# The second group of hidden column tiles in program order, its pairs' work in four steps, and two norm row operations placed later

## The chip, the core and the metric

The kernel runs on one core of a Trainium2 chip. The metric is the device time of one execution in microseconds (us). Four engines work here: TensorE (PE in the profile; its weight loads are PEld), VectorE (DVE), ScalarE (ACT) and GpSimd (POOL, almost idle). SyncE (SP) issues the loads. Each engine runs its own instructions in their order and waits on semaphores for the others.

## The reference

One encoder layer on 256 tokens of width 2048 in float32: attention, cross-attention to 256 memory tokens, and an MLP, each followed by a layer norm. The change lies in the MLP and at its entrance:

```python
x = layer_norm(ALPHA * x + xa, ln2_g[l], ln2_b[l])
ff = squared_relu_mlp(x, w_mlp_in[l], w_mlp_out[l])   # square(relu(h @ w_in)) @ w_out
x = layer_norm(ALPHA * x + ff, ln3_g[l], ln3_b[l])
```

The MLP's hidden width is 8192, that is 64 column tiles of 128.

## The kernel before, in words

**Splits.** Every float32 operand is split into a high and a low half: ScalarE copies the source to `hi` (in the reduced format that TensorE multiplies), VectorE subtracts to get `lo` (lines 87 and 88; in the stage studied, `queued_split` at lines 947 to 949). A product takes three matmuls, hi·hi, hi·lo and lo·hi (`mm3`, lines 164 to 166). Weights arrive in 1 MB loads (`raw`), and each load becomes two halves of 128x1024, each with its own pair of splits. `w_hi` has four buffers and `lo` four fixed ones, so a split also waits until TensorE has used the buffer four halves back.

**The groups.** The first eight column tiles of the hidden layer are computed ahead, in two groups of four (`hidden_group`, line 970). A group goes over the 16 row tiles k of the width; `cols_wide` (line 208) issues, for each k, four matmuls of 128x512 with `hi` (line 213) and four of 128x256 with `lo` (line 218). One half of a load covers two values of k. Group 1 writes the four `acc` tiles, group 2 the four `att` tiles. After a group its tiles are emptied (`evacuate`, lines 870 and 871), and two tiles make a **pair** p. `finish` applies relu (879) and the square (880) to a pair and splits it into `ht` (874, 875); `pair_sums` makes three sums of its quarters on VectorE (891, 894, 895) and splits those into `aux` (874, 875).

**The passes.** After that the kernel runs passes over (chunk c, half q). A pass alternates a **g** item (`hidden_tile`, lines 1004 and 1012: one more column tile of the hidden layer, 16 wide and 16 narrow matmuls) with a **u** item (a pair multiplied into the output, seven products by a Strassen scheme, 21 matmuls at lines 164 to 166, on four splits: two from `raw`, two from the sums `s_t` that line 941 makes). In the first pass the order is g8, g9, u0, g10, u1, g11, u2, g12, and so on; u0 and u1 use the pairs of group 1, u2 and u3 those of group 2.

**What sets the order.** `queue` (line 100) ties an instruction behind the last one queued on its engine. Splits of the groups and passes are queued on ScalarE and VectorE, and the g and u matmuls on TensorE. Before the change the matmuls of group 2 are in free order: a scheduler places them. Work beside the splits stands in the list `side`; `pump` (line 110) takes entries from it, two after each half in group 2, and in the passes one after each split that has no sum of `s_t` to make. The entries of group 1 are: four empty ones, two evacuations, then `finish` and `pair_sums` of each pair as whole entries, then four row operations `norm_ops(0)` (line 1174: the layer norm's gain, then its bias, on the residual, 128x1024 each, for two row blocks). Those of group 2 are two evacuations, `finish`, `pair_sums`, `finish`, `pair_sums`, taken up in g8 and u0. `norm_rows` (1168) loads the gain and bias rows into `row_b`, again with the other half of the columns once the first four row operations are done.

```python
    side.extend([lambda i=i, h=h: empty(i, h) for i, h in pairs])
    for i, h in pairs:
        side.append(lambda i=i, h=h: finish(h, c, j0 // 2 + i, queue))
        side.append(lambda i=i, h=h: pair_sums(h, c, j0 // 2 + i, queue))
```

Of the kernel before, what the change touches and what calls it, by code (L numbers as in the profile page):

```python
# [14 lines left out]
AF = mybir.ActivationFunctionType  # L15
# [3 lines left out]
P = 128  # L19
S = 256  # L20
D = 2048
KT = D // P
# [11 lines left out]
CH = 16  # L34
# [4 lines left out]
def encoder_kernel(ctx: ExitStack, tc: tile.TileContext, t, out):  # L39
    nc = tc.nc  # L40
# [29 lines left out]
    def tmp_tile():  # L70
        return rings["tmp"].tile([P, 512], F32, tag="tmp", name="tmp")
# [10 lines left out]
    def pin(ins, pinned):  # L82
        return tc.keep_in_program_order(ins) if pinned else ins
# [18 lines left out]
    side, banks, fixed_lo = deque(), deque(), deque()  # L102
# [105 lines left out]
    def cols_wide(outs, hi, lo, xt, k, nk, pinned=False):  # L208


        def his():
            for i, ps in enumerate(outs):
                pin(nc.tensor.matmul(ps, hi[:, i * P:(i + 1) * P], xt[:, k, :],  # L213
                                     start=k == 0, stop=k == nk - 1), pinned)

        def los():
            for i, ps in enumerate(outs):
                pin(nc.tensor.matmul(ps[:, 0:S], lo[:, i * P:(i + 1) * P], xt[:, k, 0:S],
                                     start=False, stop=False), pinned)

        for part in ((los, his) if k == nk - 1 else (his, los)):
            part()
# [99 lines left out]
    class Heads:  # L322
# [11 lines left out]
        def finish(self):  # L334
            while self.live:
                self.step()
# [515 lines left out]
    def take(what, c, p):  # L852
        place[what, c, p] = free[what].pop(0)
# [19 lines left out]
    def ordered_split(hi, lo, src, to):  # L873
        to(nc.scalar.activation(hi, src, AF.Copy))
        to(nc.vector.tensor_tensor(out=lo, in0=src, in1=f(hi), op=ALU.subtract))

    def finish(h, c, p, to=free_order):

        to(nc.scalar.activation(h, h, AF.Relu))
        to(nc.scalar.activation(h, h, AF.Square))  # L880
        take("h", c, p)
        x = hid(c, p)
        ordered_split(x[:, :, 0:S], x[:, :, S:2 * S], h.rearrange("p (i c) -> p i c", c=S), to)

    def pair_sums(h, c, p, to=free_order):

        if p in SEVEN:
            a11, a21, a12, a22 = [h[:, o:o + P] for o in range(0, 4 * P, P)]
            s = tmp_tile()
            s3, s1, s2, s4 = [s[:, o:o + P] for o in range(0, 4 * P, P)]  # L890
            to(nc.vector.tensor_tensor(out=s[:, 0:2 * P].rearrange("p (i c) -> p i c", c=P),
                                       in0=a21[:, None, :].broadcast_to([P, 2, P]),
                                       in1=h.rearrange("p (i c) -> p i c", c=P)[:, 0:4:3, :], op=ALU.subtract))
            to(nc.vector.tensor_tensor(out=s2, in0=s1, in1=a11, op=ALU.subtract))
            to(nc.vector.tensor_tensor(out=s4, in0=a12, in1=s2, op=ALU.add))
            take("s", c, p)
            y = sums_of(c, p)
            ordered_split(y[:, 0, :], y[:, 1, :], s, to)

    raws, raw_of, fetched, sums = [raw_x], {}, [0], deque()  # L900
    items = []
# [68 lines left out]
    def hidden_group(nexts, tiles, c, j0, beside=None):  # L970

        outs = [tiles() for _ in range(G)]
        for k in range(0, KT, 2):
            hi, lo = nexts(k)
            for i in range(2):
                cols_wide(outs, hi[:, i * G * P:(i + 1) * G * P], lo[:, i * G * P:(i + 1) * G * P],
                          x2t, k + i, KT, beside is not None)
            if beside is not None:
                beside(k // 2)
        if j0 + G == LEAD:  # L980
            for _ in range(3):
                fetch()
        pairs = [(i // 2, tmp_tile()) for i in range(0, G, 2)]

        def empty(i, h):
            for j in range(2):
                evacuate(outs[2 * i + j], h, j, queue)

        side.extend([lambda i=i, h=h: empty(i, h) for i, h in pairs])
        for i, h in pairs:  # L990
            side.append(lambda i=i, h=h: finish(h, c, j0 // 2 + i, queue))
            side.append(lambda i=i, h=h: pair_sums(h, c, j0 // 2 + i, queue))

    now, late_finish = [], []

    def hidden_tile(it, ps):

        _, c, j = it
        for h_ in range(2):
            hi, lo = part(raw_of[it][:, h_ * 1024:(h_ + 1) * 1024])  # L1000
            k0 = 8 * h_

            def w_hi(k):
                queue(nc.tensor.matmul(ps, hi[:, k * P:(k + 1) * P], x2t[:, k0 + k, :],  # L1004
                                       start=k0 + k == 0, stop=k0 + k == KT - 1))
# [12 lines left out]
        evacuate(ps, now[0], j % 2)  # L1018
        if j % 2:
            def rest(h=now[0]):  # L1020
                last = j == CH - 1
                finish(h, c, j // 2, queue if last else free_order)
                pair_sums(h, c, j // 2)
            late_finish.append(rest)

    bank = []
# [139 lines left out]
    def norm_rows(q):  # L1166
        for i, w in enumerate("gb"):
            nc.sync.dma_start(row_b[:, i * 1024:(i + 1) * 1024],
                              t[f"ln2_{w}"][q * 1024:(q + 1) * 1024].partition_broadcast(P))

    def norm_ops(q):
        o = q * 1024
        return [lambda i=i, b=b, op=op: queue(
            nc.vector.tensor_tensor(out=res[b][:, o:o + 1024], in0=res[b][:, o:o + 1024],
                                    in1=row_b[:, i * 1024:(i + 1) * 1024], op=op))
            for i, op in enumerate((ALU.mult, ALU.add)) for b in range(NB)]

    for g in range(LEAD // G):
        hidden_group((lambda k: w_mi0[k // 2]) if g == 0 else (lambda k: s_in.next()),
                     att_tile if g % 2 else acc_tile, 0, g * G, first_pair if g == 0 else None)  # L1180
        if g == 0:
# [150 lines left out]
```

## Time and profile before

| | |
|---|---|
| median of 3 runs | 1109.28 us (1107.59 to 1109.54) |
| the profiled execution's own time | 1109.07 us |
| its span | 1107.3 us |
| TensorE busy | 98% of the span |
| VectorE busy | 85% |
| ScalarE busy | 58% |
| group 2, g8, g9, u0, g10, u1 | 423.28 to 487.87 us |

The times of the trace count from the start of the span. A timeline row gives the start, the duration from the first to the last end of what it merges, the engine, the line, the operation, output and inputs, a count, and in brackets the idle time of the engine just before and what ended it. Durations of neighbours overlap, because the engines are pipelined: what an instruction costs its engine is the distance from its start to the next start. A windows row gives for one stretch the busy time of each engine, the granted TensorE clock (1.00 is full), the share of the DMA engines and GB/s.

### The profile page before, as it was taken

What the parts mean: (1) busy time and instruction counts of PE and PEld (TensorE: products, weight loads), DVE (VectorE), ACT (ScalarE), POOL (GpSimd) and SP (SyncE); (2) the same over time, 40 slices, a digit from 0 to 9 for tenths busy, and PEclk for the clock granted to TensorE, in tenths of its full rate; (3) what the DMA queues carried; (4) which work ended last, traced back from release to release, by engine and by line L of the source; (5) the groups of instructions that cost most, each with busy time, mean ns of one, the idle gap of its engine ahead of it and who ended that gap; (6) DMA issues with size and microseconds to landing.
All of it is one profiled execution on the core that took longest, in us unless ns stands there. A gap on an engine that the chain in (4) does not pass through costs nothing.

```text
span 1107.3 us, 15277 instructions
## 1 busy us (share of the span) xinstructions
PE 1082.2 (98%) x5864; PEld 932.2 (84%) x5864; DVE 936.7 (85%) x1299; ACT 638.5 (58%) x925; POOL 38.2 (3%) x45
## 2 busy tenths in 40 slices
PE   9999999999999999889999999999999999999996
PEld 6988899988999877768888888888888888888885
DVE  6878677687889676899999999899999899999876
ACT  6555566545576425566566566566666566666540
POOL 1402000000100000000000000000000000000000
PEclk9999999999999999999999999999999999999998
DMA  9664453466567334645566556556655555645742
GB/s 332 235 228 143 156 194 124 178 218 244 184 200 277 140 113 152 228 152 198 193 217 228 195 186 226 192 190 209 210 190 195 211 192 197 226 167 196 256 147 77
DMA packets 37369, 215.87 MB, mean 195 GB/s; under 512 B 4272, under 2 KB 5168, under 8 KB 13616
## 3 DMA queue, kind: packets, MB, share of 16 engines
q1 hardware_dynamic: 37296, 214.89, 54.7%
q8 instruction: 46, 0.75, 0.3%
q14 instruction: 27, 0.22, 0.1%
HBM read 212.78 MB, written 2.10 MB: 194 GB/s over the span
## 4 chain that ended last, share of the span: by engine, by line
PE 89%; DVE 6%; ACT 2%; DMA 2%; issue 1%; SPq 0%; POOL 0%; DVEq 0%; ACTq 0%
PE acc L164 12%; PE acc L165 12%; PE acc L166 12%; PE acc L1004 11%; PE acc L1012 6%; PE att L1004 6%; PE att L165 4%; PE att L166 4%; PE att L164 4%; PE att L1012 3%; PE acc L206 2%; PE acc L205 2%; PE acc L204 2%; DVE lo L949 2%; PE acc L213 1%; PE att L213 1%
## 5 line engine op out<-in xcount | busy, mean ns | idle before, releaser
L87 ACT ACTIVATE w_hi<-raw 128x1024 fp32r<-128x1024 f32 (+2 forms) x134 | 131.6, 989 | 114.1 <-PE acc L166 73.3
L88 DVE TENSOR_TENSOR w_lo<-raw,w_hi 128x1024 fp32r<-128x1024 f32 (+2 forms) x130 | 146.0, 1132 | 59.5 <-ACT w_hi L87 58.5
L949 DVE TENSOR_TENSOR lo<-raw,w_hi 128x1024 fp32r<-128x1024 f32 (+1 forms) x154 | 171.2, 1128 | 6.2 <-ACT w_hi L948 5.9
L948 ACT ACTIVATE w_hi<-raw 128x1024 fp32r<-128x1024 f32 (+1 forms) x154 | 147.5, 982 | 29.4 <-PE acc L166 27.0
L1004 PE MATMUL acc<-x2t,w_hi 128*128 128x512 f32 x592 | 153.6, 391 | 1.5 <-ACT w_hi L948 1.4
L1004 PEld LDWEIGHTS acc<-x2t,w_hi 128*128 128x128 f32 x592 | 108.8, 189 | 21.7 <-ACT w_hi L948 2.1
L949 DVE TENSOR_TENSOR lo<-s_t,w_hi 128x1024 fp32r<-128x1024 f32 x84 | 102.5, 1220 | 12.0 <-ACT w_hi L948 12.0
L948 ACT ACTIVATE w_hi<-s_t 128x1024 fp32r<-128x1024 f32 x84 | 88.8, 1057 | 35.2 <-PE acc L1004 11.8
L1012 PEld LDWEIGHTS acc<-x2t,lo 128*128 128x128 f32 x592 | 80.7, 190 | 5.8
L165 PE MATMUL acc<-lo,ht 128*128 128x512 f32 x213 | 82.9, 389 | 0.0
L1012 PE MATMUL acc<-x2t,lo 128*128 128x256 f32 x592 | 82.5, 282 | 0.0
L164 PE MATMUL acc<-w_hi,ht 128*128 128x512 f32 x210 | 82.0, 391 | 0.2 <-DVE res L1075 0.2
L166 PE MATMUL acc<-w_hi,ht 128*128 128x512 f32 x210 | 81.8, 389 | 0.0
L1004 PE MATMUL att<-x2t,w_hi 128*128 128x512 f32 x304 | 78.4, 391 | 0.0
L870 ACT ACTIVATE tmp<-acc 128x256 f32<-128x256 f32 x41 | 15.6, 388 | 102.1 <-PE acc L1004 95.2
L165 PE MATMUL acc<-w_lo,xt 128*128 128x512 f32 (+2 forms) x192 | 69.4, 363 | 0.6 <-DVE w_lo L88 0.6
L166 PE MATMUL acc<-w_hi,xt 128*128 128x512 f32 (+2 forms) x192 | 69.1, 361 | 0.0
L164 PE MATMUL acc<-w_hi,xt 128*128 128x512 f32 (+2 forms) x192 | 65.7, 362 | 0.7 <-ACT w_hi L87 0.7
L1004 PEld LDWEIGHTS att<-x2t,w_hi 128*128 128x128 f32 x304 | 55.8, 189 | 10.0
L949 DVE TENSOR_TENSOR lo<-raw_x,w_hi 128x1024 fp32r<-128x1024 f32 (+1 forms) x50 | 55.2, 1122 | 2.4 <-ACT w_hi L948 2.4
L164 PE MATMUL att<-w_hi,aux 128*128 128x512 f32 x131 | 51.3, 392 | 2.5 <-ACT w_hi L948 2.3
L165 PE MATMUL att<-lo,aux 128*128 128x512 f32 x131 | 51.3, 392 | 2.1 <-DVE lo L949 2.1
(293 smaller groups left out, 2505.7 us busy)
## 6 DMA issues: line engine op xcount, KB each, us to landing
raw<-in_w_mo SPq DMA_DIRECT2D x41, 1024.0 KB, 4.9
raw<-in_w_mc SPq DMA_DIRECT2D x34, 1024.0 KB, 4.9
raw<-in_w_out SPq DMA_DIRECT2D x16, 1024.0 KB, 4.8
raw_x<-in_w_mc SPq DMA_DIRECT2D x13, 1024.0 KB, 4.8
raw_x<-in_w_mo SPq DMA_DIRECT2D x13, 1024.0 KB, 4.9
row_b<-in_w_mo SPq DMA_DIRECT2D x10, 1024.0 KB, 4.8
row_b<-in_w_mc SPq DMA_DIRECT2D x9, 1024.0 KB, 4.9
raw<-in_w_mi SPq DMA_DIRECT2D x8, 1024.0 KB, 5.0
```

The source lines that it names most:

```text
L87: pin(nc.scalar.activation(hi, src, AF.Copy), pinned)
L88: return pin(nc.vector.tensor_tensor(out=lo, in0=src, in1=f(hi), op=ALU.subtract), pinned)
L164: keep(nc.tensor.matmul(ps, ah, bh, start=start, stop=False))
L165: keep(nc.tensor.matmul(ps, ah, bl, start=False, stop=False))
L166: keep(nc.tensor.matmul(ps, al, bh, start=False, stop=stop))
L204: nc.tensor.matmul(ps, hi, xt[:, k, 0:S], start=k == 0, stop=False)
L205: nc.tensor.matmul(ps, hi, xt[:, k, S:2 * S], start=False, stop=False)
L206: nc.tensor.matmul(ps, lo, xt[:, k, 0:S], start=False, stop=k == nk - 1)
L948: queue(nc.scalar.activation(hi, src, AF.Copy))
L949: queue(nc.vector.tensor_tensor(out=lo, in0=src, in1=f(hi), op=ALU.subtract))
L1004: queue(nc.tensor.matmul(ps, hi[:, k * P:(k + 1) * P], x2t[:, k0 + k, :], start=k0 + k == 0, stop=k0 + k == KT - 1))
L1012: queue(nc.tensor.matmul(ps[:, 0:S], lo[:, k * P:(k + 1) * P], x2t[:, k0 + k, 0:S], start=False, stop=False))
```

## The change

1. The matmuls of group 2 are queued from its third row tile on (k > 1), and the last row tile of group 1, which was only kept in program order, is queued as well. TensorE therefore runs the rest of group 1 before the rest of group 2, and the whole of group 2 before g8.
2. `finish` and `pair_sums` become four steps, `square`, `halve`, `add` and `halve_sums`, and these are listed by hand: in group 1 one entry after another with the two gain row operations among the last; in group 2 a list whose entries hold up to two steps.
3. The two bias row operations move from group 2 behind group 2's own pairs, which puts them into u1; the load of the next gain and bias rows follows them in the list, so these two loads stand later in SyncE's order, with loads of weights between them.

```diff
+        def order_of(k):
+            if beside is None:
+                return queue if k > 1 else free_order
+            if k < KT - 1:
+                return lambda ins: pin(ins, True)
+            return lambda ins: queue(pin(ins, True))
...
-        side.extend([lambda i=i, h=h: empty(i, h) for i, h in pairs])
-        for i, h in pairs:
-            side.append(lambda i=i, h=h: finish(h, c, j0 // 2 + i, queue))
-            side.append(lambda i=i, h=h: pair_sums(h, c, j0 // 2 + i, queue))
+        todo = [stages(h, c, j0 // 2 + i, queue) for i, h in pairs]
+        return [lambda i=i, h=h: empty(i, h) for i, h in pairs], todo
...
         if g == 0:
             norm_rows(0)
-            side.extend(norm_ops(0))
-            side.extendleft([lambda: None] * 4)
+            rows = norm_ops(0)
+            (a1, a2, a3, a4), (b1, b2, b3, b4) = first, second
+            side.extend(wait * 4 + empty + [a1, b1, a3, a2, a4, b3, b2, rows[0], b4, rows[1]])
             s_in.split, s_in.beside = queued_split, 2
         else:
-            norm_rows(1)
+            (a1, a2, a3, a4), (b1, b2, b3, b4) = first, second
+            assert not side
+            side.extend(wait + both(*empty) + [a1] + both(a3, a2) + [a4, b1] + both(b3, b2) + [b4] + rows[2:] + [lambda: norm_rows(1)])
```

In `stages`, step 1 is `square` (relu and square), 2 `halve` (into `ht`), 3 `add` (three sums), 4 `halve_sums` (into `aux`).

TensorE where group 1 ends, as a difference (`acc` is group 1, `att` group 2; lines with a minus stood there before, those with a plus stand there now):

```order
 L213 MATMUL att<-x2t,w_hi 128x512 x4
 L218 MATMUL att<-x2t,lo_4186 128x256 x4
+L213 MATMUL acc<-x2t,w_hi 128x512 x4
+L218 MATMUL acc<-x2t,lo_4189 128x256 x8
+L213 MATMUL acc<-x2t,w_hi 128x512 x4
 L213 MATMUL att<-x2t,w_hi 128x512 x4
 L218 MATMUL att<-x2t,lo_4187 128x256 x4
 L213 MATMUL att<-x2t,w_hi 128x512 x4
-L218 MATMUL att<-x2t,lo_4187 128x256 x2
-L213 MATMUL acc<-x2t,w_hi 128x512 x4
-L218 MATMUL acc<-x2t,lo_4189 128x256 x8
-L213 MATMUL acc<-x2t,w_hi 128x512 x4
```

The last two row tiles of group 1 moved ahead of one half of group 2.

ScalarE in group 2 before, from the split of its fourth half (`w_hi_4475`) to the seventh (`w_hi_4558`):

```order
L948 ACTIVATE w_hi_4475<-raw_4446 128x1024
L879 ACTIVATE tmp_4398<-tmp_4398 128x512
L880 ACTIVATE tmp_4398<-tmp_4398 128x512
L874 ACTIVATE ht_4184<-tmp_4398 128x2x256
L874 ACTIVATE aux_4185<-tmp_4482 128x512
L948 ACTIVATE w_hi_4506<-raw_4504 128x1024
L879 ACTIVATE tmp_4399<-tmp_4399 128x512
L880 ACTIVATE tmp_4399<-tmp_4399 128x512
L874 ACTIVATE ht_4184<-tmp_4399 128x2x256
L874 ACTIVATE aux_4185<-tmp_4513 128x512
L948 ACTIVATE w_hi_4535<-raw_4504 128x1024
L948 ACTIVATE w_hi_4558<-raw_4556 128x1024
```

And the same stretch now (lines 883 and 884 are relu and square, 955 is the split):

```order
L955 ACTIVATE w_hi_4475<-raw_4446 128x1024
L883 ACTIVATE tmp_4398<-tmp_4398 128x512
L884 ACTIVATE tmp_4398<-tmp_4398 128x512
L883 ACTIVATE tmp_4399<-tmp_4399 128x512
L884 ACTIVATE tmp_4399<-tmp_4399 128x512
L955 ACTIVATE w_hi_4500<-raw_4498 128x1024
L874 ACTIVATE ht_4184<-tmp_4398 128x2x256
L955 ACTIVATE w_hi_4525<-raw_4498 128x1024
L874 ACTIVATE aux_4185<-tmp_4503 128x512
L955 ACTIVATE w_hi_4552<-raw_4550 128x1024
L874 ACTIVATE ht_4184<-tmp_4399 128x2x256
L955 ACTIVATE w_hi_4574<-raw_4550 128x1024
```

Both pairs' relu and square now stand ahead of the fifth half's split, and one split into `ht` or `aux` between any two of the splits after it.

VectorE in u1 before, from its first split (`w_hi_4820`) to the first of g11 (`w_hi_4854`):

```order
L949 TENSOR_TENSOR lo2_4188<-raw_x_4192,w_hi_4820 128x1024
L949 TENSOR_TENSOR lo3_4189<-raw_x_4192,w_hi_4829 128x512
L949 TENSOR_TENSOR lo0_4186<-s_t_4191,w_hi_4835 128x1024
L871 TENSOR_TENSOR tmp_4815<-acc_4610,tmp_4815 128x256
L949 TENSOR_TENSOR lo1_4187<-s_t_4191,w_hi_4844 128x1024
L949 TENSOR_TENSOR lo2_4188<-raw_4599,w_hi_4854 128x1024
```

And now, from behind the first split of u1 to its last:

```order
L898 TENSOR_TENSOR tmp_4756<-tmp_4659,tmp_4756 128x128
L894 TENSOR_TENSOR tmp_4811<-tmp_4602 128x256
L871 TENSOR_TENSOR tmp_4803<-acc_4606,tmp_4803 128x256
L897 TENSOR_TENSOR tmp_4811<-tmp_4811,tmp_4602 128x128
L875 TENSOR_TENSOR aux_4185<-tmp_4756,aux_4185 128x512
L898 TENSOR_TENSOR tmp_4811<-tmp_4602,tmp_4811 128x128
L875 TENSOR_TENSOR ht_4184<-tmp_4602,ht_4184 128x2x256
L956 TENSOR_TENSOR lo3_4189<-raw_x_4192,w_hi_4823 128x512
L875 TENSOR_TENSOR aux_4185<-tmp_4811,aux_4185 128x512
L956 TENSOR_TENSOR lo0_4186<-s_t_4191,w_hi_4831 128x1024
L1186 TENSOR_TENSOR res0_1490<-res0_1490,row_b_4193 128x1024
L956 TENSOR_TENSOR lo1_4187<-s_t_4191,w_hi_4841 128x1024
```

Steps of two pairs and the bias row operations (line 1186; the second one stands behind the last row shown) moved to between the splits of u1. From g11 on the order of every engine is the same as before, but for the relu, the square and the split into `ht` of one later pair (that of g10 and g11), which stand one place later on ScalarE.

More of the change, by code (lines that the diff above doesn't have):

```diff
@@ L206, in cols_mm, with cols_wide @@
         nc.tensor.matmul(ps, lo, xt[:, k, 0:S], start=False, stop=k == nk - 1)
-    def cols_wide(outs, hi, lo, xt, k, nk, pinned=False):
+    def cols_wide(outs, hi, lo, xt, k, nk, to):
         def his():
             for i, ps in enumerate(outs):
-                pin(nc.tensor.matmul(ps, hi[:, i * P:(i + 1) * P], xt[:, k, :],
-                                     start=k == 0, stop=k == nk - 1), pinned)
+                to(nc.tensor.matmul(ps, hi[:, i * P:(i + 1) * P], xt[:, k, :],
+                                    start=k == 0, stop=k == nk - 1))
         def los():
             for i, ps in enumerate(outs):
-                pin(nc.tensor.matmul(ps[:, 0:S], lo[:, i * P:(i + 1) * P], xt[:, k, 0:S],
-                                     start=False, stop=False), pinned)
+                to(nc.tensor.matmul(ps[:, 0:S], lo[:, i * P:(i + 1) * P], xt[:, k, 0:S],
+                                    start=False, stop=False))
         for part in ((los, his) if k == nk - 1 else (his, los)):
@@ L875, in ordered_split, with stages, square, halve @@
         to(nc.vector.tensor_tensor(out=lo, in0=src, in1=f(hi), op=ALU.subtract))
[L877 to L891, printed above, removed]
+    def stages(h, c, p, to=free_order):
+        a11, a21, a12, a22 = [h[:, o:o + P] for o in range(0, 4 * P, P)]
+        s = []
+        def square():
+            to(nc.scalar.activation(h, h, AF.Relu))
+            to(nc.scalar.activation(h, h, AF.Square))
+        def halve():
+            take("h", c, p)
+            x = hid(c, p)
+            ordered_split(x[:, :, 0:S], x[:, :, S:2 * S], h.rearrange("p (i c) -> p i c", c=S), to)
+        def add():
+            s.append(tmp_tile())
+            s3, s1, s2, s4 = [s[0][:, o:o + P] for o in range(0, 4 * P, P)]
+            to(nc.vector.tensor_tensor(out=s[0][:, 0:2 * P].rearrange("p (i c) -> p i c", c=P),
                                        in0=a21[:, None, :].broadcast_to([P, 2, P]),
@@ L895, in pair_sums, with halve_sums @@
             to(nc.vector.tensor_tensor(out=s4, in0=a12, in1=s2, op=ALU.add))
+        def halve_sums():
             take("s", c, p)
             y = sums_of(c, p)
-            ordered_split(y[:, 0, :], y[:, 1, :], s, to)
+            ordered_split(y[:, 0, :], y[:, 1, :], s[0], to)
+        return [square, halve] + [add, halve_sums] * (p in SEVEN)
     raws, raw_of, fetched, sums = [raw_x], {}, [0], deque()
@@ L976, in hidden_group @@
                 cols_wide(outs, hi[:, i * G * P:(i + 1) * G * P], lo[:, i * G * P:(i + 1) * G * P],
-                          x2t, k + i, KT, beside is not None)
+                          x2t, k + i, KT, order_of(k + i))
             if beside is not None:
@@ L1020, in rest @@
             def rest(h=now[0]):
-                last = j == CH - 1
-                finish(h, c, j // 2, queue if last else free_order)
-                pair_sums(h, c, j // 2)
+                for stage in stages(h, c, j // 2, queue if j == CH - 1 else free_order):
+                    stage()
             late_finish.append(rest)
@@ L1178, in encoder_kernel, with both @@
     for g in range(LEAD // G):
-        hidden_group((lambda k: w_mi0[k // 2]) if g == 0 else (lambda k: s_in.next()),
+        empty, (first, second) = hidden_group((lambda k: w_mi0[k // 2]) if g == 0 else (lambda k: s_in.next()),
                      att_tile if g % 2 else acc_tile, 0, g * G, first_pair if g == 0 else None)
+        wait = [lambda: None]
+        def both(*todo):
+            return [lambda: [x() for x in todo]]
         if g == 0:
             norm_rows(0)
-            side.extend(norm_ops(0))
-            side.extendleft([lambda: None] * 4)
+            rows = norm_ops(0)
+            (a1, a2, a3, a4), (b1, b2, b3, b4) = first, second
+            side.extend(wait * 4 + empty + [a1, b1, a3, a2, a4, b3, b2, rows[0], b4, rows[1]])
             s_in.split, s_in.beside = queued_split, 2
         else:
-            norm_rows(1)
+            (a1, a2, a3, a4), (b1, b2, b3, b4) = first, second
+            assert not side
+            side.extend(wait + both(*empty) + [a1] + both(a3, a2) + [a4, b1] + both(b3, b2) + [b4] + rows[2:] + [lambda: norm_rows(1)])
     bank[:] = [acc_tile() for _ in range(4)] + [att_tile() for _ in range(4)]
```

## The prediction

> **What bounds the kernel now.** I read the page first, then busy times by stage, then the timeline of each engine in the one stage that is not full.
>
> ```profile
> span 1107.3 us, 15277 instructions
> PE 1082.2 (98%) x5864; PEld 932.2 (84%) x5864; DVE 936.7 (85%) x1299; ACT 638.5 (58%) x925; POOL 38.2 (3%) x45
> raw<-in_w_mc SPq DMA_DIRECT2D x34, 1024.0 KB, 4.9
> ```
>
> TensorE bounds the span: 98% busy. A change that leaves its work alone can only remove idle or slow TensorE time. The windows from the start of group 2 to the start of g11, of the two rounds behind it, and of one short piece inside, show where that lies (PE busy comes first, then PEld, DVE, ACT; the last three numbers are clock, DMA share and GB/s):
>
> ```profile
> 423.28:487.87 64.59, 56.00 (x284) 45.60 (x283) 48.95 (x70) 35.87 (x54) 0.00 (x0) 0.97 0.49 176
> 487.87:529.30 41.43, 41.43 (x214) 35.48 (x213) 39.61 (x48) 27.59 (x36) 0.00 (x0) 1.00 0.56 204
> 444.40:447.80 3.40, 3.38 (x12) 2.64 (x11) 3.40 (x4) 1.90 (x3) 0.00 (x0) 0.52 0.58 186
> ```
>
> In the changed stretch TensorE is idle for 64.59 - 56.00 = 8.6 us and for 3.4 us runs at half clock, which costs about 3.4 x 0.48 = 1.6 us. Behind it TensorE has no idle time at all, but VectorE is at 39.61 of 41.43, so it has 1.8 us to spare in four g and u rounds. That limits how much work may be pushed to there. TensorE's timeline names the waits:
>
> ```profile
> 423.28 1.09 PE L213 MATMUL att<-x2t,w_hi 128*128 128x512 f32 x4
> 426.08 1.09 PE L213 MATMUL att<-x2t,w_hi 128*128 128x512 f32 x4
> 438.34 1.18 PE L213 MATMUL att<-x2t,w_hi 128*128 128x512 f32 x4 [0.88 <-ACT w_hi L948]
> 443.51 1.23 PE L213 MATMUL att<-x2t,w_hi 128*128 128x512 f32 x4 [1.79 <-ACT w_hi L948]
> 449.11 1.99 PE L1004 MATMUL acc<-x2t,w_hi 128*128 128x512 f32 x8
> 465.26 0.40 PE L164 MATMUL att<-w_hi,ht 128*128 128x512 f32 x1
> 468.92 0.50 PE L164 MATMUL att<-w_hi,aux 128*128 128x512 f32 x1 [1.43 <-ACT w_hi L948]
> 470.18 0.50 PE L165 MATMUL att<-lo,aux 128*128 128x512 f32 x1 [0.76 <-DVE lo L949]
> 472.47 0.50 PE L164 MATMUL att<-w_hi,aux 128*128 128x512 f32 x1 [0.88 <-ACT w_hi L948]
> 473.73 0.50 PE L165 MATMUL att<-lo,aux 128*128 128x512 f32 x1 [0.76 <-DVE lo L949]
> 476.61 2.12 PE L1004 MATMUL acc<-x2t,w_hi 128*128 128x512 f32 x8 [1.45 <-ACT w_hi L948]
> 487.87 1.98 PE L1004 MATMUL acc<-x2t,w_hi 128*128 128x512 f32 x8
> 493.44 0.40 PE L164 MATMUL att<-w_hi,ht 128*128 128x512 f32 x1
> 498.22 1.98 PE L1004 MATMUL acc<-x2t,w_hi 128*128 128x512 f32 x8
> ```
>
> Every wait is for a split, two in group 2 and five in u0 (which starts at 465.26) and ahead of g10. ScalarE's timeline shows why the split at 442.42 was late:
>
> ```profile
> 430.96 1.21 ACT L870 ACTIVATE tmp<-acc 128x256 f32<-128x256 f32 x4 [6.90 <-PE acc L213]
> 437.25 1.04 ACT L948 ACTIVATE w_hi<-raw 128x1024 fp32r<-128x1024 f32 x1
> 438.19 0.62 ACT L879 ACTIVATE tmp<-tmp 128x512 f32<-128x512 f32 x1
> 438.84 0.63 ACT L880 ACTIVATE tmp<-tmp 128x512 f32<-128x512 f32 x1
> 439.51 0.63 ACT L874 ACTIVATE ht<-tmp 128x512 fp32r<-128x512 f32 x1
> 441.88 0.63 ACT L874 ACTIVATE aux<-tmp 128x512 fp32r<-128x512 f32 x1 [1.74 <-DVE tmp L895]
> 442.42 2.94 ACT L948 ACTIVATE w_hi<-raw 128x1024 fp32r<-128x1024 f32 x3
> 493.64 0.39 ACT L870 ACTIVATE tmp<-acc 128x256 f32<-128x256 f32 x1 [2.64 <-PE acc L1004]
> ```
>
> A whole pair stands between two splits, and ScalarE idles 1.74 us inside it for VectorE's sums. The splits come 5.17 us apart (437.25 to 442.42), while TensorE uses up a half in 2.80 (423.28 to 426.08).
>
> **Part 1: group 2, g8 and g9.** Costs are distances from start to start. A half of a group is 2.80 us; a g item 493.44 - 487.87 = 5.57; a u pass 498.22 - 493.44 = 4.78. From 423.28, where both kernels are still alike, there are nine halves (eight of group 2 and group 1's last) and two g items before u0: 9 x 2.80 + 2 x 5.57 = 36.34, so u0 could start at 459.6, 5.7 earlier than at 465.26.
>
> Do the splits keep up? Group 1's last matmuls move one half ahead, so its evacuation starts 2.6 to 2.8 us before the row at 430.96, near 428.3. ScalarE then does four evacuations (1.1 together), a split (0.95), two relus and two squares (0.52 to 0.67 each, 2.4) before the split of the fifth half: 428.3 + 1.1 + 0.95 + 2.4 = 432.75, and that split lands 1.04 later, at 433.8, while TensorE wants it at 423.28 + 5 x 2.80 = 437.3 (group 1's last half and four of group 2 go first). After it only one pair step of about 0.6 stands between two splits, 0.95 + 0.6 against 2.80; the steps' own waits for VectorE are under 1 us, since the sums stand ahead of them by a split. The lead of 3.5 us holds, the two waits of 0.88 and 1.79 go, and with them the slow clock behind them. Cover: if a load came late, its wait would be bare, because g8's eight matmuls (449.11) no longer fill it; a load lands in 4.9 us and the buffers of these loads come free as before or earlier, so I charge nothing. Queueing the matmuls adds no wait of its own; it only fixes the order.
>
> **Part 2: u0, g10 and u1.** Without waits g11 would start at 459.6 + 4.78 + 5.57 + 4.78 = 474.8, against 487.87. But the moved work now lies here, on VectorE. Its cadence, from a stretch without waits:
>
> ```profile
> 444.63 2.35 DVE L1174 TENSOR_TENSOR res<-res,row_b 128x1024 f32<-128x1024 f32 x2
> ...
> 498.42 1.22 DVE L949 TENSOR_TENSOR lo<-raw,w_hi 128x1024 fp32r<-128x1024 f32 x1
> 499.55 0.42 DVE L891 TENSOR_TENSOR tmp<-tmp 128x256 f32<-128x256 f32 x1
> 499.89 0.68 DVE L941 TENSOR_TENSOR s_t<-s_t,raw_x 128x512 f32<-128x512 f32 x1
> 500.49 0.68 DVE L875 TENSOR_TENSOR ht<-tmp,ht 128x512 fp32r<-128x512 f32 x1
> 501.09 0.28 DVE L894 TENSOR_TENSOR tmp<-tmp 128x128 f32<-128x128 f32 x1
> 501.29 0.68 DVE L941 TENSOR_TENSOR s_t<-s_t,raw_x 128x512 f32<-128x512 f32 x1
> 501.89 1.82 DVE L949 TENSOR_TENSOR lo<-raw_x,w_hi 128x1024 fp32r<-128x1024 f32 x2
> ```
>
> A 128x1024 operation takes 1.13 (498.42 to 499.55; a row operation the same, 2.35 - 1.22), 128x512 0.60, 128x256 0.34, 128x128 0.20 where the next does not need it. u0 itself should run free: its third split, late today, now has one pair step ahead of it and waits only for the buffer that g9's first eight matmuls free, at 459.6 - 5.57 + 1.8 = 455.8; its `hi` lands near 457 and its `lo`, with two VectorE operations between, by 460.2, and nine matmuls at 0.23 run before it is wanted, at 461.7. The chain begins when g9 ends, 459.8. ScalarE then does an evacuation (0.28), the last split of u0 (0.95), two relus and a square (3 x 0.52, now ahead of it), and g10's first split, which lands 1.04 later: 463.7. From there VectorE has, in order and without a gap, up to the start of u1's last split: six operations of 128x1024 (g10's two splits, one sum into `s_t`, u1's first and third split, one row operation), seven of 128x512, three of 128x256 and four of 128x128, 6 x 1.13 + 7 x 0.60 + 3 x 0.34 + 4 x 0.20 = 12.8. The split starts at 476.5 and lands 1.22 later, 477.7. Five matmuls of u1 wait for it, 1.25 us as after the row at 473.73. g11 starts at 479.0, not at 474.8: 4.2 us of the gain are given back, 1.13 of them for the first row operation. In u1, which starts at 470.0, TensorE will wait at each of the four splits, longest at the second: by the same count that one lands at 463.7 + 4 x 1.13 + 5 x 0.60 + 3 x 0.34 + 4 x 0.20 + 0.68 = 473.7, and seven matmuls and a first wait of 0.4 after u1's start, at 472.1, it is wanted: 1.6. The second row operation lies behind the last split and ahead of g11's first one, which lands at 476.5 + 2 x 1.13 + 1.22 = 480.0 and is wanted after g11's first eight matmuls, at 479.0 + 1.8: it costs nothing.
>
> Sum: 487.87 - 479.0 = 8.9 us.
>
> **Part 3: the clock.** The half-speed piece came at 444.4, behind waits of 0.88 and 1.79 us; the five waits from 467.5 to 476.6 were followed by none. So waits as I expect in u1 may or may not bring another one. Over the last 3.4 us of u1 it costs at most about 1.0 (VectorE's own delay hides the rest), and otherwise 0; I take 0.5, the middle, since the rows show both. The Trainium skill, "TensorE: Matmul & The Clock Gate", section "What's actually happening", has the clock halved only after an idle window of about 3.4 us. By that nothing is lost in u1, and the time would be 0.5 us less. The trace does not agree with it as written: the clock fell to 0.52 behind gaps of 1.79 and 0.88.
>
> **Part 4: behind it.** From g11 on all engines have the order they had, and VectorE's 1.8 us to spare in 41.43 means that it does not push TensorE back. A shift of 8 us should reach the end. Loads: each lands in 4.9 us, and a round of g and u, 10.35 us, needs two. The loads of the next norm rows stand later in SyncE's order, behind row operations that VectorE reaches before the splits that the next weight load waits for anyway, so nothing is queued behind them for long; they are used only in the second pass. 0.
>
> Sum: 1109.07 - 8.9 + 0.5 = 1100.7 us. The profiled execution lies 0.2 below the median of the three runs, so I take it for the median too.
>
> **The rivals.**
>
> *VectorE does not recover (8 in 100).* u2's first split lands, if VectorE goes on without a gap, at 476.5 + 5 x 1.13 + 2 x 0.60 + 1.22 = 484.6, and is wanted one matmul into u2, at 479.0 + 5.57 + 0.23 = 484.8: 0.2 in hand. If each step costs a little more than its row, u2 and u3 each wait about as long as one of u0's waits today, 0.76 to 1.43. Against it: 0.45 us per round to spare. Time: 1100.7 + 2.2 = 1102.9.
>
> *Nothing gained (3 in 100).* Should something else set the pace of the stretch, the loads above all, the waits only change their name: 1109. For it: nothing but the 98%. Against it: DMA share 0.49 in the stretch, and all waits are for splits.
>
> *Slower (3 in 100).* Group 2 in a fixed order waits barely at each half. It decides where more than 2.80 us of ScalarE's work lies between two splits and the lead of 3.5 us is used up. If the five last halves each waited 1.79, as the worst does today, that is 9.0, and three pieces at half clock add 3 x 1.6 = 4.8. u0 would then start at 459.6 + 13.8 = 473.4, and g11, 19.4 later as in part 2, at 492.8: 4.9 later than now, 1114.0. Against it: ScalarE has 1.55 us of work per half.
>
> **How the numbers follow.** The forecast has the other 86 in 100: 1100.7, and alone it reaches from 1099.0 (no slow clock, 1100.2, less most of the 1.5 by which the fastest run of before lies under the profiled one) to 1101.9 (1.0 for the clock, 0.7 for readings). With the first rival the range goes to 1102.9, and 0.5 for the spread of runs: 1099.0 to 1103.4. About 0.2%, 2.2 us, is what a measurement of this kernel can tell from no change. Forecast and first rival are both faster by more: 0.94; same 0.03; slower 0.03.
>
> **What would show it.** Right: in the new profile no TensorE idle time and full clock in group 2; u0 starting near 459.6; waits in u1 for `lo`, ended by VectorE, of 3 to 4 us together; g11 near 479.0; the stretches behind it unchanged in length. Wrong: waits for `w_hi` in group 2 (the third rival), waits in u2 or u3 (the first), or a shift at g11 that is gone by the end.

## The result and the profile after

The changed kernel takes 1100.29 us, median of 6 runs (1098.54 to 1100.9); the kernel before takes 1107.99 us, median of 6 runs (1107.5 to 1109.54). The ratio is 0.9924, with a 95% interval from 0.9912 to 0.9937. The change makes the kernel faster by 0.63 to 0.88%. The forecast was 1100.7.

The head of the page of after:

```profile
span 1097.0 us, 15276 instructions
PE 1078.5 (98%) x5864; PEld 932.4 (85%) x5864; DVE 936.8 (85%) x1299; ACT 638.4 (58%) x925; POOL 35.6 (3%) x45
```

The profiled execution took 1098.77 us. The work of VectorE and ScalarE is the same as before to 0.1 us, and TensorE has the same 5864 matmuls. What went is idle and slow time of TensorE. The windows show where (busy time of PE, PEld, DVE, ACT, then POOL, clock, DMA share and GB/s). The first is the stretch from the start of group 2 to the start of g11, which is 423.28 to 487.87 in the profile before; the second the two rounds behind it; the third a piece of u1; the last a piece ahead of group 2:

```profile
421.38:477.65 56.27, 53.71 (x285) 45.51 (x283) 47.21 (x69) 35.98 (x54) 0.00 (x0) 0.97 0.53 193
477.65:519.08 41.43, 41.43 (x214) 35.48 (x213) 40.23 (x49) 27.62 (x36) 0.00 (x0) 1.00 0.61 216
473.60:477.00 3.40, 3.31 (x9) 2.67 (x10) 3.40 (x5) 2.32 (x3) 0.00 (x0) 0.56 0.66 272
400.00:403.50 3.50, 3.50 (x23) 3.10 (x22) 2.91 (x8) 1.13 (x2) 0.00 (x0) 1.00 0.00 0
```

The stretch is 56.27 us long instead of 64.59. TensorE's idle time in it fell from 8.6 to 56.27 - 53.71 = 2.6 us. The rounds behind it take 41.43 us as before. There is again a piece at about half clock, but it now lies in u1.

The last row holds a difference that the change did not make. In the profile before, the same place ran at half clock:

```profile
400.00:403.50 3.50, 3.50 (x11) 2.89 (x11) 3.13 (x7) 0.84 (x2) 0.00 (x0) 0.52 0.00 0
```

In 3.50 us TensorE has 11 matmuls there and 23 in the profile of after, from code that both kernels share. The cost can be read from the distance between group 1's first matmul, at 399.83 before and 399.45 after, and group 2: it is 423.28 - 399.83 = 23.45 us before and 421.38 - 399.45 = 21.93 in the profile of after, with 133 matmuls and no idle time in either. These 1.52 us are most of the 423.28 - 421.38 = 1.90 us by which group 2 starts earlier in the profile of after. From g11 to the end of the span it is 619.43 us before and 1097.0 - 477.65 = 619.35 after. So the two profiled executions, 1109.07 - 1098.77 = 10.30 apart, differ by 1.90 ahead of the change, by 8.32 in the stretch, and by 0.08 behind it. Only the 8.32 belongs to the change. A second profile of the changed kernel, below, has the slow piece near 400 as before had it, and is 8.43 from before.

TensorE's timeline of after, in the stretch (the steps of the prediction in order: group 2, u0, g10, u1, g11):

```profile
421.38 1.08 PE L213 MATMUL att<-x2t,w_hi 128*128 128x512 f32 x4
...
457.77 0.40 PE L164 MATMUL att<-w_hi,ht 128*128 128x512 f32 x1
...
462.55 1.98 PE L1017 MATMUL acc<-x2t,w_hi 128*128 128x512 f32 x8
...
468.12 0.40 PE L164 MATMUL att<-w_hi,ht 128*128 128x512 f32 x1
468.88 0.50 PE L165 MATMUL att<-lo,ht 128*128 128x512 f32 x1 [0.36 <-DVE lo L956]
...
471.95 0.50 PE L165 MATMUL acc<-lo,ht 128*128 128x512 f32 x1 [1.44 <-DVE lo L956]
...
473.69 0.80 PE L165 MATMUL att<-lo,aux 128*128 128x512 f32 x1 [0.77 <-DVE lo L956]
474.28 0.63 PE L166 MATMUL att<-w_hi,aux 128*128 128x512 f32 x1
...
477.65 1.98 PE L1017 MATMUL acc<-x2t,w_hi 128*128 128x512 f32 x8
```

The two waits in group 2 and all five from u0 to g10 are gone. Three waits are left, all in u1, all for `lo` on VectorE. From the third on, single matmuls show 0.63 us, where they show 0.39 at full clock: the half clock, which begins at 473.18, inside the third wait.

VectorE's timeline of after, from the first split of g10, with which the predicted chain begins, to the last split of u1:

```profile
461.84 1.23 DVE L956 TENSOR_TENSOR lo<-raw,w_hi 128x1024 fp32r<-128x1024 f32 x1 [1.28 <-ACT w_hi L955]
...
473.55 1.22 DVE L1186 TENSOR_TENSOR res<-res,row_b 128x1024 f32<-128x1024 f32 x1
474.68 1.22 DVE L956 TENSOR_TENSOR lo<-s_t,w_hi 128x1024 fp32r<-128x1024 f32 x1
```

From 461.84 to the split at 474.68 VectorE has no gap; the next three waits of TensorE are waits for this chain. ScalarE's timeline of after shows the splits of group 2, from the evacuation of group 1 on:

```profile
426.49 1.21 ACT L870 ACTIVATE tmp<-acc 128x256 f32<-128x256 f32 x4 [4.32 <-PE acc L213]
...
430.91 1.04 ACT L955 ACTIVATE w_hi<-raw 128x1024 fp32r<-128x1024 f32 x1
...
432.38 1.04 ACT L955 ACTIVATE w_hi<-raw 128x1024 fp32r<-128x1024 f32 x1
434.24 0.63 ACT L874 ACTIVATE aux<-tmp 128x512 fp32r<-128x512 f32 x1 [0.81 <-DVE tmp L898]
434.77 1.05 ACT L955 ACTIVATE w_hi<-raw 128x1024 fp32r<-128x1024 f32 x1
```

One step of a pair lies between two splits, and these come 1.5 and 2.4 us apart (430.91, 432.38, 434.77), under the 2.80 us in which TensorE uses up a half.

### The profile page after: what moved, and what is told of

Read it like the earlier page. It is cut to its first block, busy times and chain, and to the rows that moved or that the text cites. A ratio compares the mean times of both kernels' runs of the same rounds, so it can differ in the third digit from the quotient of the medians.

```text
span 1097.0 us, 15276 instructions
## 1 busy us (share of the span) xinstructions
PE 1078.5 (98%) x5864; PEld 932.4 (85%) x5864; DVE 936.8 (85%) x1299; ACT 638.4 (58%) x925; POOL 35.6 (3%) x45
## 4 chain that ended last, share of the span: by engine, by line
PE 93%; DVE 5%; ACT 1%; issue 1%; DMA 0%; POOL 0%; DVEq 0%; SPq 0%
PE acc L164 13%; PE acc L165 13%; PE acc L166 13%; PE acc L1017 12%; PE acc L1025 6%; PE att L1017 6%; PE att L165 4%; PE att L166 4%; PE att L164 4%; PE att L1025 3%; PE acc L206 2%; PE acc L204 2%; PE acc L205 2%; DVE lo L956 1%; PE acc L213 1%; PE att L213 1%
## 5 line engine op out<-in xcount | busy, mean ns | idle before, releaser
L955 ACT ACTIVATE w_hi<-raw_x 128x1024 fp32r<-128x1024 f32 (+1 forms) x50 | 47.9, 976 | 10.2 <-PE acc L166 5.2
```

The source lines that it names most:

```text
L955: queue(nc.scalar.activation(hi, src, AF.Copy))
```

## The experiments

"The stretch" is the time from group 2's start to g11's start in an experiment's profile: 64.59 before, 56.27 after. It is used beside the medians, since it leaves out the slow piece near 400, which comes in some executions and not in others.

**1. The four steps and the row operations alone.** The changed kernel, with the matmuls of group 2 left to the scheduler as before:

```
-                return queue if k > 1 else free_order
-            if k < KT - 1:
-                return lambda ins: pin(ins, True)
-            return lambda ins: queue(pin(ins, True))
+                return free_order
+            return lambda ins: pin(ins, True)
```

> The changed kernel with group 2's matmuls left in free order, so group 1's last half runs one half of group 2 later; the four steps and the moved row operations stay. My theory: the fifth half's split then lands near 436.5 instead of 433.8 (times on the clock of the profile before), still ahead of 437.3, so group 2 has no wait, u0 starts near 459.6 and the time is that of the changed kernel, ratio to before 0.992 to 0.994. Rival (the order of the matmuls is what pays, the steps only follow): the two waits for w_hi in group 2 stay, at least 2.5 us and a half-clock piece, and the ratio is 0.996 or more.

Measured: 1099.81 us (1099.1 to 1100.45), ratio 0.9921 (0.9907 to 0.9935), by its median the same as the whole change. The stretch is 56.90. TensorE has no wait in group 2, and u0 starts 36.42 us after it (after: 36.39). The waits of TensorE, one in u0 and four in u1, of which the first and the last are shown:

```profile
460.81 0.50 PE L165 MATMUL att<-lo,aux 128*128 128x512 f32 x1 [0.58 <-DVE lo L956]
...
477.00 0.50 PE L165 MATMUL att<-lo,aux 128*128 128x512 f32 x1 [0.62 <-DVE lo L956]
```

The five add up to 3.5 us, and no piece at half clock follows. The order of the work on ScalarE and VectorE carries 64.59 - 56.90 = 7.7 of the 8.3 us by itself. The stretch is 0.6 longer than that of after, though after ran a part of u1 at half clock; experiment 7, which did not, has 55.85.

**2. The program order alone.** The kernel before, with `order_of` and the queued matmuls of the change:

```
-    def cols_wide(outs, hi, lo, xt, k, nk, pinned=False):
+    def cols_wide(outs, hi, lo, xt, k, nk, to):
...
+        def order_of(k):
+            if beside is None:
+                return queue if k > 1 else free_order
+            if k < KT - 1:
+                return lambda ins: pin(ins, True)
+            return lambda ins: queue(pin(ins, True))
```

> The kernel before with only the matmuls of group 2 in program order; whole pairs as entries, all four row operations in group 2. My theory: evacuation starts 2.6 us earlier, so the wait at the fifth half goes and that at the sixth shrinks from 1.79 to about 0.8, but the row operations now delay two lo splits by 0.6 to 0.7 each; u0 starts about 3.3 us earlier than before, and the waits of u0 and g10 (5.8 us) stay: ratio about 0.997, 3 us of the 8. With e1 the parts overlap in group 2, so they sum to more than the whole. Rival (order pays): 6 us or more, ratio 0.9945. Third rival of the prediction (bare waits in a fixed order): slower than before.

Measured: 1104.32 us (1102.71 to 1107.21), ratio 0.9963 (0.9951 to 0.9975), a gain of about 0.0037 x 1109 = 4.1 us. TensorE's waits:

```profile
439.34 1.19 PE L213 MATMUL att<-x2t,w_hi 128*128 128x512 f32 x4 [0.69 <-ACT w_hi L948]
444.00 0.74 PE L218 MATMUL att<-x2t,lo 128*128 128x256 f32 x4 [0.34 <-DVE lo L949]
447.40 1.21 PE L218 MATMUL att<-x2t,lo 128*128 128x256 f32 x8 [0.33 <-DVE lo L949]
463.76 0.50 PE L164 MATMUL att<-w_hi,aux 128*128 128x512 f32 x1 [1.00 <-ACT w_hi L948]
...
471.46 2.11 PE L1012 MATMUL acc<-x2t,w_hi 128*128 128x512 f32 x8 [1.46 <-ACT w_hi L948]
```

In group 2 the waits of 0.88 and 1.79 became 0.69, 0.34 and 0.33, and no slow piece follows them. The waits from u0 to g10 are those of before, but for the first, which is 1.00 and not 1.43, and u1 has one of 0.50. So this part gains by itself, and the two parts overlap: the stretch is 61.03, so alone 2 gains 64.59 - 61.03 = 3.6 us in it and 1 gains 7.7, but together they gain 8.3. Both take away the waits of 0.88 and 1.79 in group 2, and only the steps take away the five behind it.

**3. All four row operations ahead of the evacuations of group 1.** This prices the row operation in u1 (1.13 us in the prediction):

```
-            side.extend(wait * 4 + empty + [a1, b1, a3, a2, a4, b3, b2, rows[0], b4, rows[1]])
+            side.extend(wait * 4 + both(*rows[:2]) + both(*rows[2:]) + empty + [a1, b1, a3, a2, a4, b3, b2, b4])
...
-            side.extend(wait + both(*empty) + [a1] + both(a3, a2) + [a4, b1] + both(b3, b2) + [b4] + rows[2:] + [lambda: norm_rows(1)])
+            side.extend(wait + both(*empty) + [a1] + both(a3, a2) + [a4, b1] + both(b3, b2) + [b4] + [lambda: norm_rows(1)])
```

> The changed kernel with all four row operations run while VectorE waits for group 1 to end (two entries of two, ahead of the evacuations). My theory: VectorE's chain in u1 loses 1.13 us, the waits in u1 fall from about 3.7 to about 2.6, g11 starts 1.1 earlier, and 0.5 more where the half-clock piece goes too: 1.1 to 1.6 us under the changed kernel, ratio to before 0.9910 to 0.9915 where the changed kernel has 0.9924. Rival (where the row operations stand does not matter, the splits wait for ScalarE): the same as the changed kernel.

Measured: 1099.76 us (1099.28 to 1100.06), ratio 0.9919 (0.9906 to 0.9933), and a stretch of 56.51. The time expected did not come: the stretch is not shorter than the 56.27 of after. The waits in u1 are 0.35, 1.42 and 0.77, as in after, and a piece at half clock follows them, from 474.25 to 477.66. The row operation lies only ahead of the fourth split, and TensorE at half clock is too late for that split with the row operation or without it.

**4. The two bias row operations left out.** The same list as the second one of experiment 3, without `rows[2:]`, and the first list as in after. This kernel leaves the bias of the first half out of the residual.

> The changed kernel without the two bias row operations of the first half of the columns (that bias is left out of the residual). It prices them where they stand: my theory 1.13 us for the one inside the chain, nothing for the second, as e3: ratio 0.9910 to 0.9915. Rival: both cost, 2.3 us, ratio 0.990. Other rival: hidden, 0.9924 as the changed kernel.

Measured: 1099.54 us (1098.23 to 1100.83), ratio 0.9916 (0.9903 to 0.9928), and a stretch of 54.98. TensorE in u1, and then the window from behind the third wait to g11:

```profile
469.59 0.50 PE L165 MATMUL att<-lo,ht 128*128 128x512 f32 x1 [0.35 <-DVE lo L956]
472.67 0.50 PE L165 MATMUL acc<-lo,ht 128*128 128x512 f32 x1 [1.42 <-DVE lo L956]
474.41 0.50 PE L165 MATMUL att<-lo,aux 128*128 128x512 f32 x1 [0.78 <-DVE lo L956]
```

```profile
474.30:477.08 2.78, 2.67 (x12) 2.18 (x13) 2.78 (x4) 2.63 (x3) 0.00 (x0) 1.00 0.83 339
```

The three waits are those of after to 0.02 us, and yet the clock stays at 1.00. The same waits are followed by the slow piece in one execution and not in another; the last section shows what differs. With the clock full, the fourth split is there in time without the row operation. The stretch is 55.85 - 54.98 = 0.87 shorter than in experiment 7, which has the row operations and also ran u1 at full clock.

**5. Row operations early, and the second pair one entry later.** Experiment 3, with the list of group 2's pairs changed so that the second pair's relu and square, and all behind them, come one entry later:

```
-            side.extend(wait + both(*empty) + [a1] + both(a3, a2) + [a4, b1] + both(b3, b2) + [b4] + [lambda: norm_rows(1)])
+            side.extend(wait + both(*empty) + [a1] + both(a3, a2) + [a4] + wait + [b1] + both(b3, b2) + [b4] + [lambda: norm_rows(1)])
```

> The rows of e3 early, and the second pair of group 2 one entry later in the list, so that ScalarE makes g10's first split before that pair's relu and square. My theory: VectorE's chain to u1's last split begins 1.3 us earlier and is 1.13 shorter; counted from the start of group 2, g11 starts at 53.3 us (changed kernel 56.3 in its profile, 54.98 in e4's), with waits of 1 us or less in u1 and no half-clock piece: 2 to 2.5 us under the changed kernel of this call, ratio to before near 0.990. Rival (the chain is bound by what u1 itself needs, not by its beginning): as e3, 56 us and no gain.

Measured: 1096.75 us (1096.29 to 1098.42) against 1109.36 for before, ratio 0.9892 (0.9877 to 0.9907). The stretch is 53.56. TensorE from u1 to g11:

```profile
468.94 0.40 PE L164 MATMUL att<-w_hi,ht 128*128 128x512 f32 x1
...
472.77 0.50 PE L165 MATMUL att<-lo,aux 128*128 128x512 f32 x1 [1.39 <-DVE lo L956]
...
475.75 1.98 PE L1017 MATMUL acc<-x2t,w_hi 128*128 128x512 f32 x8
```

One wait is left of three, u1 takes 6.81 us instead of 477.65 - 468.12 = 9.53, and no slow piece follows. Nothing in the rest of the kernel moved: g11 to the end is 1095.2 - 475.75 = 619.45 us. This version is faster than both kernels.

**6. The second pair later, the row operations as in the change.** The list of group 2's pairs as in experiment 5, with `rows[2:]` behind `[b4]`, and the first list as in after.

> The changed kernel with only the second pair of group 2 one entry later; the bias row operations then stand behind u1's last split and inside u2. My theory: g11 at 53.3 us from the start of group 2 as in e5, but u2 waits about 0.5 us for its third split: 1.5 to 2 us under the changed kernel. Rival (the first rival of the prediction, VectorE does not recover): u2 and u3 wait 1 us or more each and the gain is lost.

Measured: 1098.69 us (1096.97 to 1100.18), ratio 0.9906 (0.9891 to 0.9921), and a stretch of 53.57, the same as in 5. So the second pair's later place shortens the stretch, and taking the row operations out of it as well adds nothing. But time is lost in the round behind it. TensorE in u2, and the row operation on VectorE:

```profile
478.01 2.00 PE L1017 MATMUL acc<-x2t,w_hi 128*128 128x512 f32 x8
...
486.64 0.50 PE L165 MATMUL att<-lo,aux 128*128 128x512 f32 x1 [0.16 <-DVE lo L956]
...
489.36 0.84 PE L1017 MATMUL acc<-x2t,w_hi 128*128 128x512 f32 x3
```

```profile
483.62 1.22 DVE L1186 TENSOR_TENSOR res<-res,row_b 128x1024 f32<-128x1024 f32 x1
484.76 0.69 DVE L956 TENSOR_TENSOR lo<-raw,w_hi 128x512 fp32r<-128x512 f32 x1
```

The second row operation now stands ahead of a split of u2. From g11 to g12 it is 489.36 - 478.01 = 11.35 us, where the rounds of before take 498.22 - 487.87 = 10.35. The expectation was 0.5. This is the mechanism of the prediction's first rival: behind g11 VectorE has next to no time to spare, and one more operation of 1.13 us there costs TensorE 1.0.

**7. The waits of u1 filled.** The changed kernel, with matmuls by a zero matrix put ahead of the matmuls that wait in u1: six at the second split, three each at the third and the fourth. They add zero to the sum:

```
+                for _ in range(fill):
+                    queue(nc.tensor.matmul(ps, zeros, ones[:, None, :].broadcast_to([P, 4, P]),
+                                           start=False, stop=False))
...
+                        mm(ps, x, hi, lo, 6 if u1 and ps is x11 else 3 if u1 and (ps is p5 or ps is p6) else 0)
```

> The changed kernel with matmuls by a zero weight, which add nothing, put where TensorE waits in u1: six of 128x512 at the second split, three each at the third and the fourth (2.6 us of work in waits of about 3). If the half-clock piece of the changed kernel comes from these waits, it is gone: full clock throughout and g11 at 55.8 us from the start of group 2 instead of 56.3. If it comes from elsewhere (a fixed place in the run), the piece stays near 473 to 477 us. If the added matmuls are too many, g11 comes later than 56.3.

Measured: 1100.47 us (1098.6 to 1100.79), ratio 0.992 (0.9908 to 0.9932), and a stretch of 55.85. TensorE in u1 (line numbers are two higher in this kernel; L1081 are the added matmuls), then the window over the second half of u1:

```profile
470.46 0.40 PE L166 MATMUL att<-w_hi,ht 128*128 128x512 f32 x1
471.21 0.50 PE L167 MATMUL att<-lo,ht 128*128 128x512 f32 x1 [0.36 <-DVE lo L958]
...
472.72 1.47 PE L1081 MATMUL acc<-ones,zeros 128*128 128x512 bf16 x6
...
475.11 0.82 PE L1081 MATMUL att<-ones,zeros 128*128 128x512 bf16 x3
...
479.56 1.75 PE L1019 MATMUL acc<-x2t,w_hi 128*128 128x512 f32 x7
```

```profile
474.00:478.00 4.00, 3.79 (x16) 1.96 (x15) 4.00 (x5) 4.00 (x5) 0.00 (x0) 1.00 0.69 223
```

TensorE still comes to the splits when VectorE is done, but the clock is full. The stretch is 56.27 - 55.85 = 0.42 shorter than in the first profile of after. That this one execution had no slow piece does not by itself prove that the filling keeps it away, since experiment 4 had none either.

**8. The changed kernel once more,** with nothing edited, for a second profile.

> The changed kernel once more, beside the others of this call: ratio to before near 0.9924. A second profile of the same program shows what varies: by my theory only the half-clock pieces, which come and go with the phase of the clock's monitor (near 400 us, and in u1), 1.7 us or less each; the waits in u1 stay within 0.1 us.

Measured: 1100.64 us (1098.67 to 1102.22), ratio 0.9922 (0.9907 to 0.9936); the profiled execution took 1100.64. The stretch, the place near 400, and the end of u1:

```profile
423.08:479.45 56.37, 53.82 (x284) 45.56 (x283) 47.33 (x69) 35.99 (x54) 0.00 (x0) 0.97 0.54 192
400.00:403.50 3.50, 3.50 (x12) 2.92 (x11) 2.93 (x7) 0.64 (x2) 0.00 (x0) 0.52 0.00 0
475.00:478.50 3.50, 3.11 (x7) 2.51 (x8) 3.50 (x4) 2.42 (x3) 0.00 (x0) 0.51 0.71 281
```

The stretch repeats to 0.1 us. The slow piece near 400 is there this time, and group 2 starts at 423.08, not at 421.38: of the 1.87 us between the two executions of one kernel, 1.70 lie ahead of the change.

**9 and 10. The waits near 400 filled,** in the changed kernel (9) and in the version of experiment 5 (10). Six and thirteen matmuls whose results are overwritten stand ahead of the two waits, of 0.71 and 1.57 us, that TensorE has there in every profile without them:

```
     scale2(1, 0)
+    fill2(6)
     turn2(1, 0)
     turn2(1, 1)
+    fill2(13)
     convert(0)
```

> The changed kernel with extra matmuls whose results are overwritten (N of 256, about 0.11 us each) on TensorE in the two waits ahead of group 1: 6 in the wait of 0.71 and 13 in the wait of 1.57 at about 398 us. Theory: the scatter of the runs, and most of the difference between the 1098.77 and the 1100.64 of the two profiled executions of the changed kernel, is the piece at half clock from 400 to 403.5, which comes in some executions and costs 1.7 us. With the waits filled it doesn't come: no slow window near 400, median 1098.7 (1098.2 to 1099.1), a spread under 1 us, ratio 0.9907. Rival: the scatter has another cause; then the median stays at 1100.4 with runs from 1098.5 to 1102. Second rival: the extra matmuls run past the waits and push the start of group 1 back, by up to 0.4.

> Four row operations early and the second pair one entry later, as in the fastest run so far (1096.75, 1096.29 to 1098.42), with the same extra matmuls ahead of group 1. Theory: no piece at half clock near 400, the one wait of 1.4 in u1, median 1096.4 (1096.0 to 1096.9), no run above 1097.2, ratio 0.9886. Rival (scatter from elsewhere): median 1096.8 with single runs above 1098.

Measured: 9 takes 1099.68 us (1098.63 to 1100.18), ratio 0.9915 (0.9901 to 0.9928); 10 takes 1096.71 us (1096.35 to 1097.03), ratio 0.9888 (0.9874 to 0.9901). The place near 400 in 9, and the end of u1:

```profile
400.00:403.50 3.50, 3.50 (x23) 3.11 (x22) 2.91 (x8) 1.13 (x2) 0.00 (x0) 1.00 0.02 5
474.00:477.40 3.40, 3.40 (x9) 2.61 (x9) 3.40 (x4) 2.23 (x3) 0.00 (x0) 0.52 0.59 248
```

And in 10, the place near 400 and the stretch:

```profile
400.00:403.50 3.50, 3.50 (x22) 3.11 (x23) 3.22 (x7) 1.23 (x3) 0.00 (x0) 1.00 0.02 5
421.83:475.42 53.59, 52.12 (x285) 44.56 (x284) 47.75 (x70) 36.13 (x54) 0.00 (x0) 1.00 0.60 212
```

Neither profile has the slow piece near 400. Kernel 10 came out as expected: its runs lie within 0.7 us, those of 5 within 2.1. Kernel 9 is 1.0 above the forecast of 1098.7, and its runs still spread over 1.55 us, though no longer up to 1102. So the piece near 400 is likely a part of the scatter of the runs, going by five and four of them, and not all of it; what else scatters in 9, whose u1 still has its waits, is not settled.

## Why the prediction was right, step by step

**Part 1, group 2 to u0: right.** The forecast was 36.34 us from group 2's start to u0; the profile has 457.77 - 421.38 = 36.39, with no wait and full clock. The working on ScalarE holds as well: the fifth half's split was put at 432.75, which is 430.85 in a trace that is 1.90 us earlier, and it starts at 430.91. The reason given for the lead, one step between two splits, is the one that the first experiment confirms. The prediction left open what the program order is worth. By experiment 1, where the steps are dealt out, nothing that the medians show, and 0.5 to 0.6 us in the stretch (56.90 against 56.37 and 56.27; 1.05 against the 55.85 of experiment 7, where u1 ran at full clock too); by experiment 2, 4.1 us where they are not.

**Part 2, VectorE's chain: right.** It was to begin 4.1 us after u0's start and begins 461.84 - 457.77 = 4.07 after it. Its 12.8 us of work up to u1's last split are 474.68 - 461.84 = 12.84. The waits at the first two splits were to be 0.4 and 1.6, and are 0.36 and 1.44. Without a slow clock u1 lost 479.56 - 470.46 - 4.78 = 4.32 us in experiment 7, against the 4.2 that the prediction gives back.

**Part 3, the clock: the reason was right, the size came out by luck.** The 0.5 was the middle between a piece of at most 1.0 and none, so it was the cost of neither case. The slow piece came in both profiles of the changed kernel, and it cost 56.27 - 55.85 = 0.42 and 56.37 - 55.85 = 0.52 us. As argued, VectorE's delay hides the rest. From the matmul that ends the third wait to g11 it is 477.65 - 473.69 = 3.96 us in after, against 477.08 - 474.41 = 2.67 in experiment 4, at full clock and without a wait at the fourth split: 1.29 are lost at half clock. In experiment 7, at full clock and with the fourth split as late as here, it is 479.56 - 476.03 = 3.53: 0.86 of the 1.29 go in return for the wait at the fourth split, which the prediction expected. That is why the three waits add up to 2.57 us and not to "3 to 4": the sign named in the prediction was wrong in this, and the time was not.

**The price of the row operation: too large.** "1.13 of it for the first row operation" is 0.87 at full clock (experiments 4 and 7) and nothing at half clock (experiment 3), since there another delay ends last. The sum did not depend on it, because the row operation was counted inside the chain of 12.8.

**Part 4 and the rivals.** From g11 to the end it is 619.35 us against 619.43. No wait stands in u2 or u3, so the first rival did not come; experiment 6 shows that it was 1.1 us of VectorE's work away. The waits did not just change their name (the second), and group 2 has none (the third).

**The sum.** -8.9 + 0.5 = -8.4 was forecast for the stretch, and the two profiles have 56.27 - 64.59 = -8.32 and 56.37 - 64.59 = -8.22. The medians are 1107.99 - 1100.29 = 7.70 us apart in the result and 1109.36 - 1100.64 = 8.72 in the runs of experiment 8; the runs of both kernels scatter by 2 to 3.5 us. The start of the sum, 1109.07, was an execution with the slow piece near 400, which the prediction did not look at, and lies 1.08 above the median 1107.99. The gain of 8.4 is 0.7 above the 7.70 of the medians. These two differences cancel in part, so that 1100.7 lies only 0.4 from 1100.29 is partly luck; the stretch is the better test.

## What to carry to other kernels

Where the bounding engine waits for splits, look at what stands between two of them in the queue of the engine that makes them: work dealt out in pieces shorter than the consumer's time per split took away waits that a fixed order of the consumer took away only in part. Work that is moved has to end up where the other engine has time to spare, so walk that engine's queue from the point at which its gaps end, and move the work on where the walk ends behind the consumer. Executions can differ ahead of the change, so compare stretches that begin where both programs are still alike.

## What the runs showed of the clock

Pieces of about 3.4 us at half clock come behind waits that are far shorter than that, or begin inside the last of them, and they come in some executions of a program and not in others. Near 400 each costs 1.3 to 1.6 us: from group 1's first matmul to group 2 it is 23.29 to 23.51 us in the four profiles that have the piece there and 21.88 to 21.96 in the eight that do not. The waits near 400 are 0.71 and 1.57 in all ten profiles in which they were not filled; in four of these the slow piece follows (before and experiments 6, 7 and 8), in six it does not. In u1, at waits of 0.35, 1.42 and 0.77, it comes in four profiles (both of the changed kernel and experiments 3 and 9) and not in one (experiment 4). Where the waits were filled with matmuls that do nothing useful, it never came, in three cases (experiments 7, 9 and 10). At those rates three such cases would come by chance 0.6 x 0.6 x 0.2 = 7 times in 100.

The traces show more than these counts. Within one execution the clock falls only at moments that lie a whole number of 3.413 us apart: in before at 400.17, 444.54 (13 x 3.413 later) and, once TensorE has stopped for good, 1099.90 (205 x 3.413 later), and likewise to 0.03 us in the six other profiles with a piece. These moments cut the time into windows, and where they lie against the program differs from one execution to the next. Here are the window ahead of the piece in after and the piece itself, and then the two windows over the same waits in experiment 4, counted back from the fall of the clock at its end:

```profile
469.77:473.18 3.41, 1.72 (x7) 0.77 (x5) 3.41 (x7) 2.45 (x4) 0.00 (x0) 1.00 0.15 22
473.18:476.59 3.41, 2.90 (x7) 2.35 (x8) 3.41 (x4) 2.33 (x4) 0.00 (x0) 0.50 0.75 291
469.77:473.19 3.42, 2.00 (x8) 1.28 (x9) 3.42 (x9) 2.38 (x4) 0.00 (x0) 1.00 0.19 77
473.19:476.60 3.41, 2.63 (x11) 1.87 (x11) 3.41 (x5) 3.39 (x4) 0.00 (x0) 1.00 0.79 286
```

TensorE is idle for 3.41 - 1.72 = 1.69 us in the first of these windows. In experiment 4 the same waits come 0.72 us later and fall into two windows, with 1.42 and 0.78 us. Each of the nine pieces follows a window in which TensorE was idle for 1.69 to 2.28 us, and none follows a window with 1.57 us or less. This also fits the filled waits, whose windows near 400 and in u1 have 0.36 us or less. It was found in the traces afterwards, and no run was made to test it. It is not the whole rule either: at the end of the kernel, windows with 1.73 us (experiment 9) and 1.91 us (experiment 4) are not followed by a fall.

The Trainium skill, "TensorE: Matmul & The Clock Gate", section "What's actually happening", has the clock decided over a window of 3.4 us that runs freely, and so may lie differently in each execution. The traces agree: the falls lie whole numbers of 3.413 us apart, and differently against the program in each execution. The section's table has the clock fall only after a window of idleness, and with that the traces do not agree: the windows ahead of these pieces were idle for 1.69 to 2.28 of 3.41 us, and the longest single wait in them is 1.79. The Trainium skill, on the same page, section "A second HAM failure mode: psum-queue depth-cycling", tells of short idle times that make the clock go up and down, and the traces agree in that no wait ahead of these pieces lasts a whole window.
